# GpSimd's weight subtraction in four pieces a unit, in the mixers and the first feed-forward units

## The chip, the cores and the metric

The kernel runs on one core of a Trainium2 chip. The core has five engines with queues of their own: TensorE (PE in the profile; PEld is its weight load), VectorE (DVE), ScalarE (ACT), GpSimd (POOL) and SyncE (SP, which here only issues DMAs). They meet at semaphores. The metric is the device time of one execution in microseconds, the median of several runs.

## The reference, cut to what matters

A diffusion backbone of four layers works on 256 latent tokens and 256 context tokens of width 1024. The token mixer of layer i is of kind i % 3: windowed attention (layers 0 and 3), latent attention (layer 1), a bidirectional linear recurrence (layer 2). Each mixer is followed by a gated feed-forward with a convolution of three taps. Everything is float32.

```
for layer in range(DEPTH):                       # 4
    kind, idx = layer % N_MIXERS, layer // N_MIXERS
    ...
    h_lat = modulate(rmsnorm(x, norm1[layer]), sh1, sc1)
    h_ctx = modulate(rmsnorm(ctx, norm1[layer]), csh1, csc1)
    ...                                          # y_lat, y_ctx = mixer(h_lat, h_ctx, its weights)
    x = x + g1 * y_lat
    x = x + g2 * conv_ffn(modulate(rmsnorm(x, norm2[layer]), sh2, sc2),
                          ffn_w_up[layer], ffn_conv_w[layer], ffn_conv_b[layer], ffn_w_down[layer])
    if with_ctx_out:                             # the same for ctx, in all layers but the last
        ...

def conv_ffn(h, w_up, conv_w, conv_b, w_down):
    gate, val = jnp.split(h @ w_up, 2, axis=-1)
    gate = depthwise_conv(gate, conv_w, conv_b, FFN_CONV // 2)
    return (jax.nn.silu(gate) * val) @ w_down
```

## The kernel before

**Products in three terms.** Float32 matrix products are made of three products in the format fp32r. Each operand is split into a high part (the value rounded to fp32r) and a low part (what is left); `mm3` (L221 to L227) adds high times high, high times low and low times high in PSUM, lines L224, L225 and L226.

**Weight units.** The weights come as 367 units in the order of `unit_plan`, nearly all of 128 x 1024 numbers (the latent attention has 15 of 384 to 864 columns). `load` issues one DMA of a unit into a buffer `raw` (three of them) on SP's queue; `convert` lets ScalarE write the high part `whi` (L214) and GpSimd subtract it from `raw` to get the low part `wlo` (L215). `whi` and `wlo` have three buffers each. So GpSimd's queue is almost only this: 367 subtractions, 44 subtractions of 128 x 256 for a part of the normalized activations (`h_lo`, L439), and a few small ones.

**Stages.** The span is, in order: the first mixer (windowed attention, to about 280 us), the feed-forward of layer 0 (to 622), latent attention (to 930), feed-forward 1 (to 1300), the recurrence (1340 to 1510), feed-forward 2 (1550 to 1920), the last windowed attention (to 2085) and the last feed-forward. `out_tail` (L451) ends each stage: it adds the last projection to the residual `x` (L449), and interleaves with it the next norm: squares and their sums (L410, L412), the reciprocal root `rsqrt` (L262 to L271, some fifteen VectorE operations on 2 to 16 columns), the normalized activations `hn` (L434) and their split into `h_hi` (L435) and `h_lo` (L441 on VectorE, L439 on GpSimd).

**Feed-forward.** `ffn` does 22 column blocks f; each has an up unit for the gate (`fug`) and one for the value (`fuv`), and the down units `fdn` follow in groups. The first three up units (`lead`) are multiplied half by half while the norm is still being finished. From f = 1 on, VectorE also makes the modulation of the next layer, 1024 columns an operation (L373, `junk<-mw,cbc`).

**Order.** Each engine's program is fixed when the kernel is built, and each engine works in that order. A tracker of the tile framework puts a semaphore wait on each instruction that reads what another engine writes, and it tells parts of a tile apart: a reader waits for the writers of the columns that it reads.

Of the kernel before, what the change touches and what calls it, by code (L numbers as in the profile page):

```python
# [15 lines left out]
ALU = mybir.AluOpType  # L16
# [95 lines left out]
def hybrid_kernel(ctx: ExitStack, tc: tile.TileContext, xT, cc, ccT, W, modwa, modwb, modw, colv, rowv, tabs, band, out, depth=DEPTH, dbg=None):  # L112
    nc = tc.nc
# [16 lines left out]
    f32 = lambda ap: ap.bitcast(F32)  # L130
# [73 lines left out]
    def load(key):  # L204
        off, w = offs[key]
        raw = raw_p.tile([128, 1024], F32, tag="raw", name="raw")[:, :w]
        nc.sync.dma_start(raw, bass.AP(tensor=W.tensor, offset=W.offset + off, ap=[[w, 128], [1, w]]))
        return raw

    def convert(raw):  # L210
        w = raw.shape[-1]
        hi = w_p.tile([128, 1024], F32R, tag="whi", name="whi")[:, :w]
        lo = w_p.tile([128, 1024], F32R, tag="wlo", name="wlo")[:, :w]
        nc.scalar.activation(hi, raw, AF.Copy)  # L214
        nc.gpsimd.tensor_tensor(lo, raw, f32(hi), op=ALU.subtract)  # L215
        return hi, lo

    def unit(key):
        return convert(load(key))

    def mm3(ps, terms, start=True, stop=True, **kw):  # L221
        n = len(terms)
# [229 lines left out]
    def out_tail(l, part, keys, per, src, t0, nxt, bank):  # L452
# [10 lines left out]
        for z, key in enumerate(keys):  # L463
            wt = unit(key)
            for m, w in cols(z, wt):
                proj_cols(l, part, m, w, src, slice(t0, T) if z < split_at else CTX[1], bank)
                if z >= split_at:
                    held.append((m, w))
# [21 lines left out]
    def half_proj(l, key, m, units, src, t0):  # L490
        if m % 2 == 0:
            units[0] = unit((*key, 0, m // 2))
        wh, wl = units[0]
        o = (m % 2) * 4
        proj_cols(l, 16, m, [(wh[:, (o + k) * 128:(o + k + 1) * 128], wl[:, (o + k) * 128:(o + k + 1) * 128])
                             for k in range(4)], src, slice(t0, T), fl_ps)
# [26 lines left out]
    def swa(l, i, q0, nm, nxt, first=None):  # L523
# [12 lines left out]
        def proj(c, ps, lead=False, hook=None):  # L536
            late, done = [], []
            for q in range(4):
                wt = hook(q, done) if hook else None
                wh, wl = wt or unit(("qkv", i, c, q))  # L540

                def part(b, q=q, wh=wh, wl=wl):
                    return mm3(ps[b], [(hblk(hi, 2 * q + z, b), hblk(lo, 2 * q + z, b), wh[:, z * 512:(z + 1) * 512],
                                        wl[:, z * 512:(z + 1) * 512]) for z in range(2)], start=q == 0, stop=q == 3)

                if lead and q < 3:
                    part(0)
                    part(1)
                    late += [lambda part=part, b=b: part(b) for b in (2, 3)]
                    if q < 2:  # L550
                        continue
                    for f in late:
                        f()
                    continue
                for b in ps:
                    op = part(b)
                done.append(op)
# [611 lines left out]
    def first(q, done):  # L1169
        with ExitStack() as order:  # L1170
            if q > 1:
                order.enter_context(tc.issue_after(done[q - 2]))
            if q > 0:
                order.enter_context(tc.issue_after(applied[q - 1]))
            mod0_lead(q, raws[q])
            wt = convert(wkv[q] if q < 3 else load(("qkv", 0, 0, q)))
        for z, s in enumerate((1, 0)):
            op = nm.apply(s, rbs[z], range(2 * q, 2 * q + 2))
        applied.append(op)
        return wt  # L1180
# [151 lines left out]
```

## Time and profile before

| | |
|---|---|
| median of 3 runs | 2292.8 us (2292.27 to 2296.81) |
| profiled execution, its own time | 2288.72 us |
| its span, first to last instruction | 2286.9 us |
| granted TensorE clock, mean | 0.979 |
| busy: PE, DVE, ACT, POOL | 2133.3, 1628.4, 1031.6, 956.4 us |

The profiled execution is one run of its own; around its span lie 1.8 us. Busy times of PE count matmuls that overlap in a pipeline, so a busy PE is not PE at its peak. Starts are microseconds from the span's start.

### The profile page before, as it was taken

What the parts mean: (1) busy time and instruction counts of PE and PEld (TensorE: products, weight loads), DVE (VectorE), ACT (ScalarE), POOL (GpSimd) and SP (SyncE); (2) the same over time, 40 slices, a digit from 0 to 9 for tenths busy, and PEclk for the clock granted to TensorE, in tenths of its full rate; (3) what the DMA queues carried; (4) which work ended last, traced back from release to release, by engine and by line L of the source; (5) the groups of instructions that cost most, each with busy time, mean ns of one, the idle gap of its engine ahead of it and who ended that gap; (6) DMA issues with size and microseconds to landing.
All of it is one profiled execution on the core that took longest, in us unless ns stands there. A gap on an engine that the chain in (4) does not pass through costs nothing.

```text
span 2286.9 us, 32497 instructions
## 1 busy us (share of the span) xinstructions
PE 2133.3 (93%) x12084; PEld 1772.5 (78%) x12084; DVE 1628.4 (71%) x3342; ACT 1031.6 (45%) x1850; POOL 956.4 (42%) x418
## 2 busy tenths in 40 slices
PE   6989999999989998899999988899999999898999
PEld 5656788888877666888888876688888887677999
DVE  4678779777776887687879789857964457885333
ACT  4466553232246775433232356635333224575544
POOL 3231145454533002354545433344544443414887
PEclk9999999999999999999999998899999999999999
DMA  8433135555522001155556422223655552303555
GB/s 301 183 120 130 38 119 190 173 172 166 176 88 66 21 29 56 54 196 175 174 175 186 128 71 68 74 83 111 193 182 172 174 162 83 102 32 98 185 184 157
DMA packets 83884, 300.11 MB, mean 131 GB/s; under 512 B 11152, under 2 KB 12816, under 8 KB 81296
## 3 DMA queue, kind: packets, MB, share of 16 engines
q1 hardware_dynamic: 83728, 298.05, 40.2%
q8 instruction: 95, 1.56, 0.3%
q14 instruction: 61, 0.50, 0.1%
HBM read 296.97 MB, written 1.05 MB: 130 GB/s over the span
## 4 chain that ended last, share of the span: by engine, by line
PE 73%; DVE 19%; ACT 4%; issue 2%; DMA 2%; POOL 1%; SPq 0%; ACTq 0%; DVEq 0%; POOLq 0%
PE fl L225 8%; PE fl L226 8%; PE fl L224 8%; PE mm L224 7%; PE mm L226 7%; PE mm L225 7%; PE mo L225 4%; PE mo L224 4%; PE mo L226 4%; PE tp L226 2%; PE tp L224 2%; PE tp L225 2%; PE mo L697 2%; PE tp L691 2%; PE mm L884 2%
## 5 line engine op out<-in xcount | busy, mean ns | idle before, releaser
L215 POOL TENSOR_TENSOR wlo<-raw,whi 128x1024 fp32r<-128x1024 f32 (+3 forms) x367 | 922.4, 2516 | 1247.9 <-ACT whi L214 1212.4
L214 ACT ACTIVATE whi<-raw 128x1024 fp32r<-128x1024 f32 (+3 forms) x367 | 382.4, 1043 | 480.6 <-PE tp L225 189.9
L373 DVE SCALAR_TENSOR_TENSOR junk<-mw,cbc 128x1024 bf16<-128x1024 f32 x256 | 456.6, 1784 | 24.1 <-DMA mw<-in_modw_dram 15.8
L224 PE MATMUL fl<-h_hi,whi 128*128 128x512 f32 (+1 forms) x832 | 298.7, 360 | 10.4 <-DVE lam L958 5.9
L226 PE MATMUL fl<-h_hi,wlo 128*128 128x512 f32 (+1 forms) x832 | 298.9, 360 | 3.6 <-POOL wlo L215 3.6
L225 PE MATMUL fl<-h_lo,whi 128*128 128x512 f32 (+1 forms) x832 | 298.9, 360 | 0.4 <-POOL h_lo L439 0.2
L224 PE MATMUL mm<-h_hi,whi 128*128 128x512 f32 (+1 forms) x768 | 271.1, 353 | 3.1 <-ACT h_hi L435 2.7
L226 PE MATMUL mm<-h_hi,wlo 128*128 128x512 f32 (+1 forms) x768 | 270.1, 352 | 3.7 <-POOL wlo L215 3.7
L225 PE MATMUL mm<-h_lo,whi 128*128 128x512 f32 (+1 forms) x768 | 269.6, 352 | 0.8 <-POOL h_lo L439 0.2
L1109 DVE SCALAR_TENSOR_TENSOR conv<-mm,colt,conv 128x510 f32<-128x510 f32 (+1 forms) x88 | 59.8, 680 | 190.3 <-ACT conv L1107 190.3
L224 PEld LDWEIGHTS fl<-h_hi,whi 128*128 128x128 f32 x832 | 158.8, 192 | 34.2 <-issue 6.0
L1113 ACT ACTIVATE conv<-conv 128x512 f32<-128x512 f32 (+1 forms) x88 | 51.0, 580 | 287.4 <-DVE conv L1111 287.3
L226 PEld LDWEIGHTS fl<-h_hi,wlo 128*128 128x128 f32 x832 | 159.0, 191 | 27.2 <-POOL wlo L215 4.6
L225 PEld LDWEIGHTS fl<-h_lo,whi 128*128 128x128 f32 x832 | 159.1, 191 | 23.5 <-POOL h_lo L439 0.6
L224 PE MATMUL mo<-g_hi,whi 128*128 128x256 f32 (+1 forms) x488 | 165.4, 339 | 9.8 <-DVE x L449 6.8
L224 PEld LDWEIGHTS mm<-h_hi,whi 128*128 128x128 f32 x768 | 147.2, 192 | 23.3 <-ACT h_hi L435 3.7
L225 PE MATMUL mo<-g_lo,whi 128*128 128x256 f32 (+1 forms) x488 | 164.6, 337 | 0.4 <-DVE g_lo L259 0.4
L226 PEld LDWEIGHTS mm<-h_hi,wlo 128*128 128x128 f32 x768 | 146.8, 191 | 23.1 <-POOL wlo L215 4.3
L226 PE MATMUL mo<-g_hi,wlo 128*128 128x256 f32 (+1 forms) x488 | 164.4, 337 | 0.0
L225 PEld LDWEIGHTS mm<-h_lo,whi 128*128 128x128 f32 x768 | 146.3, 191 | 20.7 <-POOL h_lo L439 1.4
L449 DVE SCALAR_TENSOR_TENSOR x<-mo,modc,x 128x256 f32<-128x256 f32 x212 | 95.3, 477 | 84.2 <-PE mo L226 83.9
L224 PEld LDWEIGHTS mo<-g_hi,whi 128*128 128x128 f32 x488 | 93.1, 191 | 21.9 <-DVE x L449 7.5
(313 smaller groups left out, 4443.9 us busy)
## 6 DMA issues: line engine op xcount, KB each, us to landing
raw<-in_W_dram SPq DMA_DIRECT2D x352, 512.0 KB, 3.6
mw<-in_modw_dram SPq DMA_DIRECT2D x144, 512.0 KB, 4.2
mw<-in_modwa_dram SPq DMA_DIRECT2D x8, 1024.0 KB, 15.2
mw<-in_modwb_dram SPq DMA_DIRECT2D x16, 512.0 KB, 4.5
mw<-in_modwb_dram SPq DMA_DIRECT2D x8, 1024.0 KB, 8.6
cbc<-in_cc_dram SPq DMA_DIRECT2D x3, 1024.0 KB, 6.1
raw<-in_W_dram SPq DMA_DIRECT2D x8, 384.0 KB, 2.9
x<-in_xT_dram SPq DMA_DIRECT2D x8, 256.0 KB, 4.9
```

Of the source, the lines that this page charges most:

```text
L214: nc.scalar.activation(hi, raw, AF.Copy)
L215: nc.gpsimd.tensor_tensor(lo, raw, f32(hi), op=ALU.subtract)
L224: nc.tensor.matmul(ps, ah, bh, start=start and i == 0, stop=False, **kw)
L225: nc.tensor.matmul(ps, ah, bl, start=False, stop=False, **kw)
L226: op = nc.tensor.matmul(ps, al, bh, start=False, stop=stop and i == n - 1, **kw)
L373: nc.vector.scalar_tensor_tensor(junk, raw, 1.0, cbc[:, s], op0=ALU.mult, op1=ALU.mult, accum_out=modc[l][:, s, m:m + 1])
L449: nc.vector.scalar_tensor_tensor(X[m][:, half], ps[:, half], modc[l][:, s, part + m:part + m + 1], X[m][:, half], op0=ALU.mult, op1=ALU.add)
L691: nc.tensor.transpose(pp[:, c:c + 128], P[z][:, (2 * kp + kk) * 128:(2 * kp + kk + 1) * 128], ident)
L697: nc.tensor.matmul(po[r], v[0][:, kb, p * 128 + 64 * z:p * 128 + 64 * z + 64], pt[:, kp, (kk * 2 + z) * 128:(kk * 2 + z + 1) * 128], start ...
L884: nc.tensor.matmul(ps[:, c], d["q"][:96, 2 * hp + z, bc], d["k"][:96, 2 * hp + z, :nk], start=True, stop=True)
L1109: op = nc.vector.scalar_tensor_tensor(y3[:, :, 1:], g3[:, :, :255], cw[:, l, 0, f:f + 1], y3[:, :, 1:], op0=ALU.mult, op1=ALU.add)
L1113: nc.scalar.activation(y[:, t0:], y[:, t0:], AF.Silu)
```

## The change

`convert` gets a number of parts. With four parts the subtraction on GpSimd is issued as four instructions over a quarter of the columns each (three instructions where the width is not a multiple of 512); the high part stays one instruction on ScalarE. `unit` asks for one part for the down units (`fdn`) and for up units with f over 1, and for four elsewhere; the first units of layer 0 go through `convert` with its default, four.

```
-    def convert(raw):
+    def convert(raw, parts=4):
         w = raw.shape[-1]
         hi = w_p.tile([128, 1024], F32R, tag="whi", name="whi")[:, :w]
         lo = w_p.tile([128, 1024], F32R, tag="wlo", name="wlo")[:, :w]
         nc.scalar.activation(hi, raw, AF.Copy)
-        nc.gpsimd.tensor_tensor(lo, raw, f32(hi), op=ALU.subtract)
+        step = w // (parts if w % 512 == 0 else min(parts, 3))
+        for c in range(0, w, step):
+            cs = slice(c, c + step)
+            nc.gpsimd.tensor_tensor(lo[:, cs], raw[:, cs], f32(hi[:, cs]), op=ALU.subtract)
         return hi, lo
 
     def unit(key):
-        return convert(load(key))
+        return convert(load(key), 1 if key[0] == "fdn" or key[0][0] == "f" and key[2] > 1 else 4)
```

119 of the 367 units are cut: 104 into four pieces and 15 into three. 248 stay whole, 62 in each feed-forward. All later lines of the changed kernel stand three lines further down.

On GpSimd's queue, from the first mixer over the feed-forward of layer 0 to the latent attention, the kernel before has these rows (`wlo` is the low part of a unit, `mask` a table of the attention):

```order
L215 TENSOR_TENSOR wlo<-raw,whi 128x1024 x3
L439 TENSOR_TENSOR h_lo<-hw,h_hi 128x256 x2
L577 CAST mask<-mk 128x512 x2
L215 TENSOR_TENSOR wlo<-raw,whi 128x1024 x21
L439 TENSOR_TENSOR h_lo<-hw,h_hi 128x256 x6
L215 TENSOR_TENSOR wlo<-raw,whi 128x1024 x63
L215 TENSOR_TENSOR wlo<-raw,whi 128x864 x2
L215 TENSOR_TENSOR wlo<-raw,whi 128x576
```

In the changed kernel the same stretch of GpSimd's queue reads:

```order
L218 TENSOR_TENSOR wlo<-raw,whi 128x256 x12
L442 TENSOR_TENSOR h_lo<-hw,h_hi 128x256 x2
L580 CAST mask<-mk 128x512 x2
L218 TENSOR_TENSOR wlo<-raw,whi 128x256 x84
L442 TENSOR_TENSOR h_lo<-hw,h_hi 128x256 x6
L218 TENSOR_TENSOR wlo<-raw,whi 128x256 x4
L218 TENSOR_TENSOR wlo<-raw,whi 128x1024 x62
L218 TENSOR_TENSOR wlo<-raw,whi 128x288 x6
L218 TENSOR_TENSOR wlo<-raw,whi 128x192 x3
```

Nothing has moved past anything else; each unit of the mixer stands as its pieces, and in the feed-forward one unit of the 63 is cut behind the `h_lo` (three more, the `lead`, stand ahead of them).

On TensorE, where the first two pairs of row blocks of the first projection are multiplied (`mm` and `fl` are PSUM banks), the kernel before has, with the semaphores that each row waits for:

```order
L224 MATMUL mm<-whi,h_hi 128x512 [waits Activation_49]
L225 MATMUL mm<-wlo,h_hi 128x512 [waits Pool_49]
L226 MATMUL mm<-whi,h_lo 128x512 [waits DVE_49]
L224 MATMUL mm<-whi,h_hi 128x512 [waits Activation_49]
L225 MATMUL mm<-wlo,h_hi 128x512
L226 MATMUL mm<-whi,h_lo 128x512 [waits DVE_49]
```

And the changed kernel has there:

```order
L227 MATMUL mm<-whi,h_hi 128x512 [waits Activation_49]
L228 MATMUL mm<-wlo,h_hi 128x512 [waits Pool_49]
L229 MATMUL mm<-whi,h_lo 128x512 [waits DVE_49]
L227 MATMUL mm<-whi,h_hi 128x512 [waits Activation_49]
L228 MATMUL mm<-wlo,h_hi 128x512 [waits Pool_49]
L229 MATMUL mm<-whi,h_lo 128x512 [waits DVE_49]
```

The order is the same; a matmul waits for the pieces with the columns that it reads, so the second product has a wait of its own. The rows of VectorE, ScalarE and SP keep their order everywhere; on TensorE one product is swapped with its neighbours in two feed-forward beginnings.

## Rows read from the trace of the kernel before

**Rows 1.** The page: busy times and shares; the chain that ended last, by engine.
```profile
PE 2133.3 (93%) x12084; PEld 1772.5 (78%) x12084; DVE 1628.4 (71%) x3342; ACT 1031.6 (45%) x1850; POOL 956.4 (42%) x418
...
PE 73%; DVE 19%; ACT 4%; issue 2%; DMA 2%; POOL 1%; SPq 0%; ACTq 0%; DVEq 0%; POOLq 0%
```
**Rows 2.** Busy time by stretch: us, then PE, PEld, DVE, ACT, POOL (instructions).
```profile
60.00:200.00 140.00, 124.16 (x808) 83.53 (x808) 105.50 (x360) 80.87 (x197) 31.27 (x13) 0.98 0.42 151
...
320.00:620.00 300.00, 300.00 (x1326) 248.37 (x1325) 240.12 (x338) 94.93 (x116) 150.75 (x56) 1.00 0.55 179
...
1357.00:1510.00 153.00, 129.14 (x511) 102.47 (x511) 136.21 (x128) 95.25 (x122) 59.38 (x22) 0.90 0.25 73
```
**Rows 3.** VectorE in time, 284 to 316 us: start, length, instruction [idle before].
```profile
287.85 0.17 DVE L265 TENSOR_SCALAR rs_i<-rs_v 128x2 int32<-128x2 int32 x1
288.05 2.30 DVE L266 TENSOR_SCALAR rs_y<-rs_i 128x2 int32<-128x2 int32 x1
290.39 0.16 DVE L268 TENSOR_TENSOR rs_t<-rs_y 128x2 f32<-128x2 f32 x1
290.58 0.16 DVE L269 SCALAR_TENSOR_TENSOR rs_t<-rs_t,rs_v 128x2 f32<-128x2 f32 x1
290.66 0.42 DVE L412 TENSOR_TENSOR P<-P 128x256 f32<-128x256 f32 x1
...
293.48 2.20 DVE L412 TENSOR_TENSOR P<-P 128x256 f32<-128x256 f32 x1 [0.42 <-ACT P L410]
295.61 0.47 DVE L434 SCALAR_TENSOR_TENSOR hn<-x,scale,tp 128x256 f32<-128x256 f32 x1
...
305.91 0.61 DVE L270 SCALAR_TENSOR_TENSOR rs_y<-rs_t,rs_y 128x2 f32<-128x2 f32 x1
```
**Rows 4.** GpSimd in the same stretch.
```profile
287.93 2.40 POOL L215 TENSOR_TENSOR wlo<-raw,whi 128x1024 fp32r<-128x1024 f32 x1 [10.73 <-ACT whi L214]
293.02 2.38 POOL L215 TENSOR_TENSOR wlo<-raw,whi 128x1024 fp32r<-128x1024 f32 x1 [2.69 <-ACT whi L214]
...
305.77 0.73 POOL L439 TENSOR_TENSOR h_lo<-hw,h_hi 128x256 fp32r<-128x256 f32 x1 [1.43 <-ACT hw L438]
```
**Rows 5.** VectorE by line: ns min/median/max, first and last start.
```profile
L449 DVE SCALAR_TENSOR_TENSOR x<-mo,modc,x x212: 466/476/485, 338.8 to 2283.8; 128x256 f32<-128x256 f32 x106
...
L373 DVE SCALAR_TENSOR_TENSOR junk<-mw,cbc x256: 1204/1226/3299, 329.3 to 1892.0; 128x1024 bf16<-128x1024 f32 x128
```
**Rows 6.** VectorE in time: the first and the last blocked operation of cut units.
```profile
26.16 1.29 DVE L441 SCALAR_TENSOR_TENSOR h_lo<-hn,modc,h_hi 128x256 fp32r<-128x256 f32 x1
...
2086.59 0.35 DVE L265 TENSOR_SCALAR rs_i<-rs_v 128x2 int32<-128x2 int32 x1
```
**Rows 7.** GpSimd by line and shape: busy us, mean ns.
```profile
L215 POOL TENSOR_TENSOR wlo<-raw,whi 128x1024 fp32r<-128x1024 f32 x352 | 897.8, 2553 | 1207.5 <-ACT whi L214 1172.4 <-DVE h_lo L441 12.1 <-PE mo L226 8.0
L439 POOL TENSOR_TENSOR h_lo<-hw,h_hi 128x256 fp32r<-128x256 f32 x44 | 32.3, 735 | 71.8 <-ACT hw L438 71.7
```
**Rows 8.** GpSimd, then VectorE, 115 to 122 us: two units back to back.
```profile
116.15 4.75 POOL L215 TENSOR_TENSOR wlo<-raw,whi 128x1024 fp32r<-128x1024 f32 x2 [17.67 <-ACT whi L214]
...
116.44 2.13 DVE L268 TENSOR_TENSOR rs_t<-rs_y 128x8 f32<-128x8 f32 x1
...
119.17 1.75 DVE L269 SCALAR_TENSOR_TENSOR rs_t<-rs_t,rs_v 128x8 f32<-128x8 f32 x1
```
**Rows 9.** GpSimd, then VectorE, 1433 to 1443 us, in the recurrence.
```profile
1435.01 5.93 POOL L215 TENSOR_TENSOR wlo<-raw,whi 128x1024 fp32r<-128x1024 f32 x2 [6.22 <-ACT whi L214]
...
1435.92 2.77 DVE L1028 TENSOR_SCALAR th<-ex 128x1024 f32<-128x1024 f32 x1
1438.73 3.30 DVE L1029 SCALAR_TENSOR_TENSOR ex<-ex 128x1024 f32<-128x1024 f32 x1
```
**Rows 10.** Waits of TensorE for GpSimd: us in total, times, longest.
```profile
PE mm L226 <- POOL wlo L215: 3.7, 3, 1.2
...
PE fl L226 <- POOL wlo L215: 3.6, 2, 1.9
```

## The prediction

> **What bounds the kernel now.** The page comes first: TensorE is busy 93% of the span, and the chain that ended last runs over TensorE for 73% and over VectorE for 19%; GpSimd holds 1% of it and is busy 42% [rows 1]. By that, cutting a GpSimd instruction should change nothing. The shares are means over unlike stages, so the second view is busy time by stretch: in the middle of a feed-forward TensorE is busy 300.00 of 300 us, but in the first mixer 124 of 140, and in the recurrence 129 of 153 while VectorE has 136 [rows 2]. What VectorE loses in the mixers and around the norms can cost time; in the middle of a feed-forward it can't.
>
> The third view is VectorE's timeline beside GpSimd's. At 288.05 an operation on two columns takes 2.30 us, where its neighbours take 0.16 and 0.17 [rows 3]. A subtraction of a unit began on GpSimd at 287.93 and took 2.40 [rows 4]: the VectorE operation ends when the subtraction does, at 290.35 against 290.33. The same at 293.48: 2.20 us instead of 0.42, with a subtraction from 293.02 to 295.40 [rows 3, 4]. A short subtraction blocks for its own length only: one from 305.77 to 306.50 holds an operation of 0.15 us for 0.61 [rows 3, 4]. Which operations are held is plain from their spread: L449, with an input in PSUM, has 466 to 485 ns in all 212 cases, L373, with both inputs in SBUF, 1204 to 3299 [rows 5]. So a GpSimd subtraction has something for its whole length that a VectorE operation with its operands in SBUF needs too.
>
> I count an operation as blocked when it overlaps a subtraction and is over 0.15 us longer than the quick ones of its shape. Beside units that the change cuts there are 95, from 26.16 to 2086.59 us [rows 6], and together they lose 167 us; 80 of them, with 141 us, lie on the chain. That is the stock from which a gain could come: 1.76 us an operation.
>
> **What the change does, part by part.** (1) *Price of a piece.* A subtraction of 256 columns takes 0.735 us, one of 1024 some 2.40 [rows 4, 7]. Two back to back take 4.75 us, so each next one begins 0.05 before the other's end [rows 8]. Four pieces thus take 4 x 0.735 - 3 x 0.05 = 2.8 us: 0.4 more a unit, about 0.135 for each of the 342 added instructions, 46 us on an engine that is idle 58% of the time [rows 1]. By itself that is hidden. It is not hidden where VectorE would be held by the additional 0.4.
>
> (2) *Who goes next.* No row shows four pieces, but rows 8 have two units back to back: the operation that started at 116.44 ended at 118.57, just behind the first unit's end (116.15 + 2.40 = 118.55), and did not wait for the second, which ended at 120.90. The next contending operation, at 119.17, then waited for that end. In the recurrence, too, the two engines alternate: unit, L1028, unit, L1029 [rows 9]. So I take it that a VectorE operation waits for the rest of one piece, and the next contending operation can meet the next piece.
>
> (3) *Sum over the blocked operations.* With that rule there are three sorts. Alone: at 293.48 the first piece would end at 293.75, so the 0.42 us operation ends at 294.2 instead of 295.7; the next, L434 at 0.47 us, does not contend [rows 3]; about 1.2 to 1.5 stay. In a run: from 288.05 on L266, L268, L269 and L412 all contend, and each meets a piece; L412 starts about 287.93 + 2.8 + 3 x 0.16 = 291.2 instead of 290.7, a loss of 0.3 to 0.5. Long ones: L1028 and L1029 lose 2.1 us each now [rows 9]; each would lose 0.7, and the six pieces left fall to later operations, or into a pause in which VectorE waits for ScalarE. Going through all 95 in order, with VectorE's pauses and the arrival of units kept as they are relative to its work, I get in us gained: first mixer to 240 us -4.0, its end and the first norm (240 to 316) +5.3; latent attention to 850 -2.5, its end (850 to 966) +3.5; the way into the recurrence +4.1, the recurrence itself +12.4, its end +1.9; the norm and the beginning of the last attention +5.5, its middle -0.7, its end +3.0. Sum +28.5. With 0.10 or 0.22 us for an added piece it is 38 or 12: these are the ends of this term. On the chain lie 141 of 167 us, 84%: 24 us.
>
> (4) *TensorE's first low part.* It waits for `wlo` five times, 7.3 us in all [rows 10]. With pieces the first product can go 2.40 - 0.735 = 1.7 us earlier, so these waits nearly vanish; TensorE then soon waits for VectorE's norm instead, so I count a third, 2 us.
>
> (5) *What costs nothing.* The changed program has 192 more TensorE instructions with a wait on GpSimd. In the middle of a feed-forward, where such waits stand for every unit, TensorE has no idle time [rows 2]; if GpSimd were late, each wait would show. The buffers `raw` are freed by the last piece, 0.4 us later; GpSimd sits idle before 352 units for 1207 us, nearly all of it waiting for ScalarE's `whi` [rows 7], so that stays hidden. The two swapped products keep their 0.12 us each.
>
> Sum: 24 + 2 = 26 us. The profiled execution took 2288.7, so 2262.7; it was 4.1 under the median of the runs shown, so I forecast 2266.8 by that median, in round numbers 2267.
>
> **The rivals.** *Bigger gain.* VectorE's pauses don't stay: where it waits for ScalarE or TensorE, these waited for it before, and later pieces fall into pauses. If each blocked operation on the chain kept only the rest of one piece (80 x (1.76 - 0.45) = 105 us at most) and half of that reached the end, the gain would be 50 us: 2243. Against it: rows 3 show runs of contending operations right behind a blocked one.
>
> *No change.* The blocked time is on the chain, but TensorE, busy 129 of 153 us in the recurrence and 124 of 140 in the first mixer [rows 2], takes up the slack when VectorE gets faster, and the runs lose what the lone ones win. Within 4.6 us (0.2%, about what a measurement of this kernel can tell): 2288 to 2297.
>
> *Slower: GpSimd keeps the hold from piece to piece.* All four pieces stand ahead of a VectorE operation in their queue. If GpSimd went on to its next piece while the operation waits, it would wait for 2.8 us instead of 2.4, and the 80 on the chain would lose 0.4 each, 32 us: 2325. It decides from two pieces on: an operation passed over once waits up to 1.4, not far under the 1.76 of now. Rows 8 and 9 speak against it. The Trainium skill ("SBUF — State Buffer", section "Who interferes with whom") says that whoever issues first gets the shared port pair for the whole instruction and the other fully blocks. Read strictly by issue order, that rule gives this rival and its 2325; rows 8, where the operation got in ahead of a unit that had long been queued, bear out the rule for one instruction, but not that reading for a row of them.
>
> **How the numbers follow.** The sum above holds with a chance of 0.55; its own range, from the ends of term 3 (10 to 32 us on the chain, and 2 more), is 2259 to 2281. The bigger gain has 0.13, a small gain of 5 to 10 us 0.07, no change 0.15, slower 0.10. So faster by over 0.2%: 0.75; same 0.15; slower 0.10. The range leaves out most of the slower rival and the farther half of the bigger gain: 2240 to 2294.
>
> **What would show it.** Right: GpSimd's pieces near 0.73 us and four a unit in 2.8 or a little more; the operation at 288.05 and its fellows down from 2.3 to under 0.9 us; the longest of L412 from 2.4 to about 1.2; the recurrence shorter by about ten us; TensorE's waits for `wlo` under 3 us; the middle of the feed-forwards unchanged at 300 us. Wrong: single VectorE operations still at 2.3 us and longer beside cut units (GpSimd keeps its hold); pieces that grow to 1.5 us and more in the recurrence and TensorE waiting for `wlo` there (VectorE starves GpSimd); or blocked time that falls while the stages keep their length (the path was elsewhere).

## The result, and the profile after

The changed kernel takes 2239.5 us (median of 4 runs, 2239.5 to 2246.5) where the kernel before took 2293.1 beside it: a ratio of 0.977 with a 95% interval of 0.975 to 0.979, 53.5 us less. In a later group of runs it took 2241.5 (4 runs, 2239.0 to 2245.5) against 2293.9: 0.9775, 0.976 to 0.979. The forecast was 2267 with a range down to 2240: the sign and the mechanism held, the size was twice the forecast, and the time lies half a microsecond under the range.

The page of the changed kernel, its engines and the chain that ended last:

```profile
PE 2120.5 (95%) x12084; PEld 1762.9 (79%) x12084; DVE 1572.0 (70%) x3342; ACT 1033.3 (46%) x1850; POOL 1046.0 (47%) x760
...
PE 76%; DVE 16%; ACT 4%; DMA 2%; issue 1%; POOL 1%; SPq 0%; ACTq 0%; DVEq 0%
```

Against [rows 1] GpSimd has 342 instructions and 90 us more, VectorE 56 us less, and TensorE, for the same 12084 products, 12.8 us less. The span went from 2286.9 to 2237.8, so TensorE's idle time (span less busy) went from 153.6 to 117.3. The 49.1 us of the two profiles are thus 36.3 of idle time and 12.8 of products that ran quicker.

Busy time by stretch of the changed kernel (us, then PE, PEld, DVE, ACT, POOL with instructions, granted clock). Each stretch begins and ends at the product of TensorE with which the stretches of the kernel before do:

```profile
58.60:196.60 138.00, 125.71 (x808) 85.06 (x808) 101.54 (x360) 81.29 (x197) 39.52 (x54) 0.97 0.43 153
309.70:609.70 300.00, 300.00 (x1325) 248.45 (x1325) 240.09 (x338) 94.94 (x116) 151.92 (x56) 1.00 0.55 179
...
649.70:684.70 35.00, 32.91 (x228) 30.38 (x227) 29.03 (x79) 22.43 (x57) 19.30 (x26) 1.00 0.20 62
1306.30:1326.80 20.50, 18.50 (x128) 16.97 (x128) 19.08 (x48) 11.41 (x21) 11.98 (x16) 1.00 0.20 60
1326.80:1468.60 141.80, 123.31 (x512) 98.15 (x511) 123.63 (x132) 94.08 (x120) 93.40 (x84) 0.94 0.27 79
```

The first, second and fifth answer to [rows 2]: the first mixer 2.0 us shorter, the middle of the feed-forward 300.00 as before, the recurrence 11.2 shorter. To the third and fourth answer these two of the kernel before:

```profile
660.00:700.00 40.00, 35.54 (x228) 33.03 (x227) 32.37 (x77) 22.50 (x57) 16.89 (x13) 0.91 0.18 55
1330.00:1357.00 27.00, 20.87 (x128) 18.68 (x128) 23.77 (x52) 11.45 (x21) 9.97 (x7) 0.87 0.20 59
```

Five and 6.5 us went there. In both the granted clock was 0.91 and 0.87 before and is 1.00 now, and the same 228 and 128 products take 2.6 and 2.4 us less.

VectorE of the changed kernel where [rows 3] stand, start and length:

```profile
279.34 0.17 DVE L268 TENSOR_SCALAR rs_i<-rs_v 128x2 int32<-128x2 int32 x1
279.54 0.64 DVE L269 TENSOR_SCALAR rs_y<-rs_i 128x2 int32<-128x2 int32 x1
280.22 0.66 DVE L271 TENSOR_TENSOR rs_t<-rs_y 128x2 f32<-128x2 f32 x1
280.91 0.67 DVE L272 SCALAR_TENSOR_TENSOR rs_t<-rs_t,rs_v 128x2 f32<-128x2 f32 x1
...
284.85 0.55 DVE L415 TENSOR_TENSOR P<-P 128x256 f32<-128x256 f32 x1 [0.42 <-ACT P L413]
285.31 0.47 DVE L437 SCALAR_TENSOR_TENSOR hn<-x,scale,tp 128x256 f32<-128x256 f32 x1
```

GpSimd in the same stretch, as in [rows 4]:

```profile
279.42 3.07 POOL L218 TENSOR_TENSOR wlo<-raw,whi 128x256 fp32r<-128x256 f32 x4 [8.40 <-ACT whi L214]
284.38 3.00 POOL L218 TENSOR_TENSOR wlo<-raw,whi 128x256 fp32r<-128x256 f32 x4 [1.89 <-ACT whi L214]
```

The 2.30 us operation on two columns is 0.64 now, but its followers pay 0.66 and 0.67: this run meets a piece each. The lone operation of 2.20 us is 0.55.

### The profile page after: what moved, and what is told of

Its sections match the earlier page's. It is cut to its first block, busy times and chain, and to the rows that moved or that the text cites. A ratio compares the mean times of both kernels' runs of the same rounds, so it can differ in the third digit from the quotient of the medians.

```text
span 2237.8 us, 32872 instructions
## 1 busy us (share of the span) xinstructions
PE 2120.5 (95%) x12084; PEld 1762.9 (79%) x12084; DVE 1572.0 (70%) x3342; ACT 1033.3 (46%) x1850; POOL 1046.0 (47%) x760
## 4 chain that ended last, share of the span: by engine, by line
PE 76%; DVE 16%; ACT 4%; DMA 2%; issue 1%; POOL 1%; SPq 0%; ACTq 0%; DVEq 0%
PE fl L228 9%; PE fl L229 8%; PE fl L227 8%; PE mm L227 7%; PE mm L229 7%; PE mm L228 7%; PE mo L228 4%; PE mo L227 4%; PE mo L229 4%; PE tp L227 3%; PE tp L229 2%; PE tp L228 2%; PE mo L700 2%; PE mm L887 2%; PE tp L694 2%
## 5 line engine op out<-in xcount | busy, mean ns | idle before, releaser
L218 POOL TENSOR_TENSOR wlo<-raw,whi 128x256 fp32r<-128x256 f32 (+3 forms) x709 | 1011.4, 1448 | 1121.6 <-ACT whi L214 1086.0
L376 DVE SCALAR_TENSOR_TENSOR junk<-mw,cbc 128x1024 bf16<-128x1024 f32 x256 | 457.6, 1788 | 24.3 <-DMA mw<-in_modw_dram 14.7
L452 DVE SCALAR_TENSOR_TENSOR x<-mo,modc,x 128x256 f32<-128x256 f32 x212 | 95.4, 477 | 85.9 <-PE mo L229 85.6
```

Source lines behind the costliest of these rows:

```text
L218: nc.gpsimd.tensor_tensor(lo[:, cs], raw[:, cs], f32(hi[:, cs]), op=ALU.subtract)
L376: nc.vector.scalar_tensor_tensor(junk, raw, 1.0, cbc[:, s], op0=ALU.mult, op1=ALU.mult, accum_out=modc[l][:, s, m:m + 1])
L452: nc.vector.scalar_tensor_tensor(X[m][:, half], ps[:, half], modc[l][:, s, part + m:part + m + 1], X[m][:, half], op0=ALU.mult, op1=ALU.add)
```

## Experiments

Held time below is counted as in the prediction (VectorE operations over 0.15 us longer than the quick ones of their shape in the kernel before, beside a subtraction of weights); L376, which runs in the feed-forwards (L373 before), is left out. Idle is TensorE's. Half-clock is the sum of the stretches with a granted clock of 0.5, the lower of TensorE's two levels (1.2 GHz); in most kernels the last such stretch runs some 2 us past the span and is counted whole. All but the first two columns are from the profiled execution; diffs are against the changed kernel.

| kernel | median us | ratio to before, 95% interval | span | TensorE busy | idle | held | half-clock |
|---|---|---|---|---|---|---|---|
| before | 2293.1 | 1 | 2286.9 | 2133.3 | 153.6 | 180 | 98 |
| changed | 2239.5 | 0.975 to 0.979 | 2237.8 | 2120.5 | 117.3 | 122 | 70 |
| changed, again | 2241.5 | 0.976 to 0.979 | 2243.7 | 2125.4 | 118.3 | 119 | 85 |
| last columns first | 2251.6 | 0.979 to 0.983 | 2249.8 | 2133.0 | 116.8 | 116 | 96 |
| last columns first, again | 2246.2 | 0.977 to 0.982 | 2242.2 | 2125.3 | 116.9 | 114 | 79 |
| attention units whole | 2259.4 | 0.984 to 0.987 | 2258.5 | 2129.2 | 129.3 | 139 | 87 |
| two pieces | 2258.3 | 0.983 to 0.987 | 2261.6 | 2130.1 | 131.5 | 149 | 91 |
| eight pieces | 2236.9 | 0.971 to 0.977 | 2233.8 | 2122.8 | 111.0 | 94 | 74 |
| recurrence only | 2268.1 | 0.986 to 0.991 | 2273.4 | 2126.9 | 146.5 | 158 | 88 |
| other feed-forward units only | 2282.3 | 0.992 to 0.996 | 2279.0 | 2128.7 | 150.3 | 175 | 95 |
| all units in four | 2232.5 | 0.972 to 0.974 | 2227.1 | 2118.6 | 108.5 | 115 | 67 |
| all units in eight | 2249.1 | 0.978 to 0.982 | 2251.5 | 2146.2 | 105.3 | 84 | 74 |
| eight in the mixers, four in the feed-forwards | 2214.2 | 0.964 to 0.967 | 2213.1 | 2112.4 | 100.7 | 90 | 53 |

### Is it the shorter hold, or the earlier first columns?

The pieces are issued from the last columns to the first, so the hold is as short but TensorE's first columns come last.

```
-        for c in range(0, w, step):
+        for c in range(w - step, -1, -step):
```

> The changed kernel with the pieces of a unit issued in the opposite order, the last columns first. TensorE's first product of a unit reads the first columns, so it now waits for the whole unit again, while the holds on VectorE stay short. Theory A (the gain is VectorE's shorter blocked time: 167 us before, 108 after beside the cut units): VectorE's blocked time stays near 108 us, TensorE waits for GpSimd some 7 us again in five places, and the time is 2240 to 2247 us. Rival B (the gain is TensorE getting the first low parts earlier): most of the gain is lost, 2275 us or more.

TensorE's waits for GpSimd's low parts in this kernel (us in total, times, longest):

```profile
PE fl L229 <- POOL wlo L218: 7.4, 3, 3.7
...
PE mm L229 <- POOL wlo L218: 4.9, 3, 2.2
...
PE mo L229 <- POOL wlo L218: 3.4, 1, 3.4
...
PE mm L228 <- POOL wlo L218: 0.6, 1, 0.6
...
PE fl L228 <- POOL wlo L218: 0.2, 1, 0.2
```

They are 16.5 us, where the kernel before had 7.3 [rows 10] and the changed one has none. Yet TensorE's idle time is 116.8, that of the changed kernel; the 12 us between the two profiles are its busy time, 2133.0 against 2120.5. At 2251.6 the kernel stands far nearer to theory A than to B: most of the gain is the hold. Whether the 12 us are a cost of the late first columns or chance of the clock was asked again, beside the changed kernel itself.

> The changed kernel itself, profiled once more, for what of its gain comes back in a second execution. Theory A (of the 49 us about 36 are idle time of TensorE and 13 its higher granted clock, both effects of the shorter stops): idle 114 to 121 us, busy 2117 to 2125 us, half-clock stretches 62 to 80 us. Rival B (the clock's part is chance of one execution): idle the same, busy back at 2128 to 2134 us, half-clock stretches over 85 us.

> The four pieces issued from the last columns to the first, profiled once more beside the changed kernel. Theory A (the low parts' late first columns make TensorE stop about 9 us more, and these stops cost clock): TensorE busy 2128 to 2135 us, 2248 to 2256 us. Rival B (the 12 us between it and the changed kernel were chance of the clock in one group of executions): busy 2117 to 2125 us, 2238 to 2246 us.

The changed kernel's idle time came back (118.3), its busy time only in part: 2125.4, just over theory A's bound and 8 us under before, not 13; the half-clock stretches, 85 us, stand at B's bound. So it is between the two. The other came out at 2125.3 with 16 us of waits, and at 2246.2: just over rival B's bounds.

The mean granted clock is on record for every run, and it tells more than the two profiles. It was 0.975 to 0.981 in the 23 runs of the kernel before beside these experiments, 0.982 to 0.986 in the 8 runs of the changed kernel, and 0.979 to 0.986 in the 9 with the reversed order. Each run of the changed kernel stands above each run of the kernel before, so its higher clock is no chance of one execution; how much of it a single execution gets varies, and with it the clock's part of the gain, 8 and 13 us in the two profiles. By the ratios to the kernel before, the reversed order is 9 and 5 us behind the changed kernel, with intervals that just overlap each time. Its idle time is the same, and its clock (0.981 in the mean, against 0.984 and 0.979) lies between: what the order is worth, from nothing to some 9 us, seems to be clock.

### Do the stages with long runs lose?

The sum in the prediction had the attention mixers' long stretches as losses. Here their units stay whole (with one part as `convert`'s default, too).

```
-        return convert(load(key), 1 if key[0] == "fdn" or key[0][0] == "f" and key[2] > 1 else 4)
+        return convert(load(key), 1 if key[0] == "fdn" or key[0][0] == "f" and key[2] > 1 or key[0] in ("qkv", "mdn", "muq", "mkv") or key[0] in ("swo", "mwo") and key[-2] == 0 else 4)
```

> The changed kernel, but the units that are used inside the attention mixers (the projections and the first half of the output projection of layers 0, 1 and 3) are whole again; cut stay the second half of the output projection, the recurrence and the first feed-forward units. The ledger of the prediction gives these stages a loss by the cut (-4.0 to 240 us, -2.5 to 850 us, -0.7 in the last attention), so by it this kernel is 6 to 7 us faster than the changed one, 2233 us. The theory after the result (blocked time fell there too: losses are taken up by pauses, gains are not) says that the cut gained about 2 us before 240, 6 to 7 in the latent attention up to 850 and 1 to 2 in the last attention, so this kernel is 8 to 12 us slower than the changed one, 2248 to 2252 us.

It went the other way from the prediction's sum, and further than the other theory said: 2259.4, 20 us slower than the changed kernel, with 17 us more of held time, 12 more of idle and 9 more of TensorE's busy time. These units gain.

### How does it go with the number of pieces?

```
-    def convert(raw, parts=4):
+    def convert(raw, parts=2):
```

(and 2 for 4 in `unit`; then 8 for 4 in both, and six where the width is no multiple of 512.)

> Two pieces of 512 columns (about 1.3 us each) in the same units in place of four. Theory A: a blocked operation waits for the rest of one piece; the mean wait rises from 0.46 to about 0.8 us, the blocked time beside these units lies about halfway between 167 and 108 us, 130 to 140, and the time about halfway, 2258 to 2270 us. Rival (what counts is only that a subtraction can be interrupted once): nearly the full gain, 2245 us or less.

> The 119 units in eight pieces (six where the width is no multiple of 512) in place of four. Theory A (a held VectorE operation pays the rest of the piece it meets, and halves of 2048 columns went from about 180 us of held time to 149 with two pieces and 122 with four): a further step of the same kind, held time 95 to 110 us, TensorE idle 7 to 15 us less than in the changed kernel, 2225 to 2236 us. Rival B (runs of VectorE operations already meet one piece each, so that shorter pieces only add pieces to meet, and 400 more instructions at 0.13 us make GpSimd's low parts late): held time not under 115 us, 2240 to 2255 us.

With one, two, four and eight pieces the held time is 180, 149, 122 and 94 us: each halving takes off about 28. The idle time is 153.6, 131.5, 117.3 and 111.0: the first step returns 22 us, the last 6. (The units have 1024 columns; the 2048 in the second expectation is a slip.) With eight, the held time is one us under theory A's range, the idle time fell by 6.3 us where 7 to 15 were expected, and the 2236.9 lie between the two theories. The recurrence is 5 us shorter than in the changed kernel although TensorE now waits 6.0 us for low parts there; the beginnings of the first three feed-forwards, with their first up units in eight, are some 2 us longer each than in the kernel before. Two pieces went as theory A had it.

### Do stages stand for themselves?

```
-        return convert(load(key), 1 if key[0] == "fdn" or key[0][0] == "f" and key[2] > 1 else 4)
+        return convert(load(key), 4 if key[0][0] == "l" else 1)
```

(with one part as `convert`'s default), and the opposite half of the feed-forwards:

```
+        return convert(load(key), 4 if key[0] == "fdn" or key[0][0] == "f" and key[2] > 1 else 1)
```

(here `convert`'s default stays four, so the first four units of layer 0 are cut as well: 252 units, not the 248 of the expectation.)

> Only the units of the recurrence in four pieces, all others whole. Theory A (stages stand for themselves, what a cut unit gives is given in its own stage): the stretch from 1270 to 1510 us of the kernel before is 15 to 22 us shorter, every other stretch within 2 us of before, 2271 to 2278 us. Rival B (the gain of a stage hangs on where the stages ahead of it left the units): under 10 us in that stretch, 2283 us or more.

> The opposite half: only the 248 feed-forward units that the change leaves whole are cut in four, the 119 of the change stay whole. Theory A (the two sets add up: all units in four gave 60 us, the 119 alone 49): 8 to 13 us off, 2280 to 2285 us, all of it at the ends of the feed-forward blocks and the norms behind them. Rival B (they give only together, since the norm behind a feed-forward block runs beside units of the next mixer): within 4 us of the kernel before.

Both went by theory A. The first is 3 us under theory A's range. In its profile (an execution of 2275.2, 7 us over the median) 17.6 us come from the recurrence and the way into it (the same stretch, from 1270 on, gives 20.0 in the changed kernel); of the other stretches the first 30 us are 2.6 us longer, those from 30 to 140 us 1.0 and the last attention 1.9, the way out of the recurrence is 1.6 shorter, and the rest is within 0.2. In the second the held time of L376 fell from 146 to 42 us, and the kernel gained 13: those 104 us lie beside a TensorE that never waits. In its profile, 7.9 us shorter than that of before, the gain came at the norms behind the first three feed-forwards, some 2 to 4 us each, and 2 us came from the four units of layer 0.

### What is the best cut?

```
+        return convert(load(key), 4)
```

> All 367 units in four (or three) pieces, also those of the middle of the feed-forwards. Theory A: there TensorE has no idle time, VectorE's blocked time (146 us of L373 before) is off the path, so the time stays within 3 us of the changed kernel, 2237 to 2243 us. Rival: GpSimd, 50% busy there and alternating with the 1.2 us operations L373, gets late with the low parts, TensorE waits for it, and the time rises by 10 us or more.

> All 367 units in eight pieces (six where the width is no multiple of 512). Theory A: as with four pieces in all units (2232 us) and a further 7 to 15 us less, 2217 to 2226 us. Rival B (some 1,600 added instructions at 0.13 us are 210 us more of GpSimd, which turns late in the feed-forward blocks and makes TensorE wait there): 2235 to 2270 us.

All units in four is faster than the changed kernel, 2232.5, beyond what was expected of it. All units in eight was 67 us ahead of the kernel before at the end of the last mixer and lost 32 of them in the last feed-forward. Its busy times there, 2050 to 2210 us:

```profile
2050.00:2210.00 160.00, 160.00 (x1160) 159.07 (x1159) 44.08 (x98) 68.73 (x96) 159.94 (x384) 1.00 0.53 159
```

The same with all units in four:

```profile
2050.00:2210.00 160.00, 159.93 (x1333) 159.73 (x1333) 53.02 (x116) 78.67 (x113) 157.61 (x225) 1.00 0.62 185
```

GpSimd does 384 pieces in 159.94 us, 3.33 us a unit of eight; in four it does a unit in 2.80, and 56 units in 160 us are one each 2.86. So four pieces just keep step with TensorE there and eight don't: 1160 products instead of 1333, though TensorE is called busy throughout. That is rival B, in the one feed-forward where TensorE uses up units so fast; in the middle of the first it was 56 units in 300 us [rows 2], and the other three feed-forwards lost at most 2 us each with eight. So the next kernel has eight in the mixers and four in all feed-forwards (the first four units of layer 0 have `convert`'s default, four):

```
-        step = w // (parts if w % 512 == 0 else min(parts, 3))
+        step = w // (parts if w % 512 == 0 else min(parts, 6 if parts == 8 else 3))
...
+        return convert(load(key), 4 if key[0] == "fdn" or key[0][0] == "f" else 8)
```

> Eight pieces (six where the width is no multiple of 512) in the mixers' units, four (three) in all feed-forward units. Theory A (stages stand for themselves; eight pieces gave 67 us by the end of the last mixer and then lost 32 in the last feed-forward block, where GpSimd was busy almost throughout): that loss goes, the rest stays, 2218 to 2226 us. Rival B (eight pieces give nothing that can be measured beyond four): 2228 to 2236 us, as with four pieces in all units.

It takes 2214.2 us (2212.0 to 2215.0), under theory A's range, and is the fastest of all: 79.7 us less than before. Eight pieces in the first three feed-forwards beside four in the last were not tried.

```profile
PE 2112.4 (95%) x12084; PEld 1758.0 (79%) x12084; DVE 1445.8 (65%) x3342; ACT 1039.2 (47%) x1850; POOL 1341.1 (61%) x1885
```

## Why the prediction was right in kind and short in size

**Right: price and turn (terms 1 and 2).** Four pieces take 3.0 to 3.1 us in the norm shown above, against 2.8 worked out. GpSimd has 90 us more, not the 46 of term 1: VectorE now holds its pieces in turn, and the 440 pieces of 256 columns take 0.84 us in the mean against 0.735. That stays hidden; TensorE waits for no low part.

```profile
L218 POOL TENSOR_TENSOR wlo<-raw,whi 128x256 fp32r<-128x256 f32 x440 | 357.4, 844 | 569.2 <-ACT whi L214 538.9 <-issue 12.5 <-PE mo L700 6.3
```

VectorE gets in behind each piece. The recurrence shows it longest: here VectorE, then GpSimd, at the place of [rows 9].

```profile
1401.60 1.12 DVE L1031 TENSOR_SCALAR th<-ex 128x1024 f32<-128x1024 f32 x1
1402.74 1.65 DVE L1032 SCALAR_TENSOR_TENSOR ex<-ex 128x1024 f32<-128x1024 f32 x1
```

```profile
1400.61 7.87 POOL L218 TENSOR_TENSOR wlo<-raw,whi 128x256 fp32r<-128x256 f32 x8 [4.33 <-ACT whi L214]
```

2.77 and 3.30 us became 1.12 and 1.65, and the eight pieces of two units take 7.87 us because VectorE's operations lie between them. Single pieces grow to 1.8 us in the recurrence. That is one half of a sign of being wrong; the other half, TensorE waiting for `wlo` there, did not come. The rival in which GpSimd keeps its hold is out.

**The step that failed: term 3, the sum over the blocked operations.** It forecast 28.5 us less held time, the trace has 58.5. By stage, in us (time is the stretch's gain in the first profile and in the second):

| stage (starts of before) | forecast | held time less | time less |
|---|---|---|---|
| to 240 | -4.0 | 6.1 | 4.1, 0.8 |
| 240 to 316 | 5.3 | 6.7 | 6.3, 6.3 |
| latent attention to 850 | -2.5 | 4.2 | 5.7, 3.7 |
| 850 to 966 | 3.5 | 7.0 | 7.0, 5.9 |
| 966 to 1270 | 0 | 0 | -1.6, -2.1 |
| 1270 to 1357 | 4.1 | 4.5 | 8.7, 7.2 |
| recurrence, 1357 to 1510 | 12.4 | 14.4 | 11.3, 11.6 |
| 1510 to 1600 | 1.9 | 6.3 | 2.3, 1.8 |
| 1880 to 1960 | 5.5 | 5.6 | 2.1, 2.1 |
| 1960 to 2070 | -0.7 | 0.3 | 0.7, 1.8 |
| 2070 to 2110 | 3.0 | 3.4 | 2.8, 4.2 |
| sum | 28.5 | 58.5 | 49.4, 43.3 |

The stretches that are not listed differ from before by at most 0.4 us. In six stages the sum was good to 2 us. It failed where it booked losses, to 240 us and in latent attention, and at 850 to 966 and 1510 to 1600. No stage's held time grew. The price of one meeting was right: beside cut units 236 operations are held for 108.5 us, 0.46 each, where the prediction reckoned 0.45. The number of meetings was too high: 167 less 28.5 us at 0.46 would be 301.

The prediction's own example, the run of operations from 288.05 on, shows how. It was to lose 0.3 to 0.5 us, with L412 starting 3.3 us behind the beginning of the subtraction. Behind that L412 the kernel before has, and the changed kernel has, on VectorE and then on GpSimd:

```profile
291.07 0.48 DVE L449 SCALAR_TENSOR_TENSOR x<-fl,modc,x 128x256 f32<-128x256 f32 x1
```

```profile
281.50 0.41 DVE L415 TENSOR_TENSOR P<-P 128x256 f32<-128x256 f32 x1
281.83 0.68 DVE L273 SCALAR_TENSOR_TENSOR rs_y<-rs_t,rs_y 128x2 f32<-128x2 f32 x1
282.43 0.47 DVE L452 SCALAR_TENSOR_TENSOR x<-fl,modc,x 128x256 f32<-128x256 f32 x1
```

```profile
281.51 0.98 POOL L218 TENSOR_TENSOR wlo<-raw,whi 128x256 fp32r<-128x256 f32 x1
```

L412 started 2.73 us behind the subtraction (290.66 less 287.93), L415 starts 2.08 behind it (281.50 less 279.42). Three operations meet a piece each and end with it, so the 0.16 us of each, which the prediction added, don't come on top. L415 gets in ahead of the fourth piece and is not lengthened; the piece is, to 0.98 us. L273 then pays for that piece, and the next operation, L452, starts 3.01 us behind the subtraction where L449 started 3.14 behind it: the run gained 0.13 us.

Latent attention shows the rest. VectorE, then GpSimd, of the kernel before:

```profile
662.54 2.03 DVE L265 TENSOR_SCALAR rs_i<-rs_v 128x2 int32<-128x2 int32 x1
...
667.33 1.86 DVE L270 SCALAR_TENSOR_TENSOR rs_y<-rs_t,rs_y 128x2 f32<-128x2 f32 x1
```

```profile
662.49 2.06 POOL L215 TENSOR_TENSOR wlo<-raw,whi 128x864 fp32r<-128x864 f32 x1 [10.60 <-ACT whi L214]
667.12 2.05 POOL L215 TENSOR_TENSOR wlo<-raw,whi 128x864 fp32r<-128x864 f32 x1 [2.57 <-ACT whi L214]
```

And of the changed one:

```profile
652.21 0.78 DVE L268 TENSOR_SCALAR rs_i<-rs_v 128x2 int32<-128x2 int32 x1
653.02 0.74 DVE L269 TENSOR_SCALAR rs_y<-rs_i 128x2 int32<-128x2 int32 x1
653.80 0.72 DVE L271 TENSOR_TENSOR rs_t<-rs_y 128x2 f32<-128x2 f32 x1
...
656.88 0.64 DVE L273 SCALAR_TENSOR_TENSOR rs_y<-rs_t,rs_y 128x2 f32<-128x2 f32 x1
657.44 0.41 DVE L415 TENSOR_TENSOR P<-P 128x256 f32<-128x256 f32 x1
658.32 0.48 DVE L437 SCALAR_TENSOR_TENSOR hn<-x,scale,tp 128x256 f32<-128x256 f32 x1 [0.47 <-PE tp L427]
```

```profile
652.16 2.34 POOL L218 TENSOR_TENSOR wlo<-raw,whi 128x288 fp32r<-128x288 f32 x3 [10.60 <-ACT whi L214]
656.66 2.63 POOL L218 TENSOR_TENSOR wlo<-raw,whi 128x288 fp32r<-128x288 f32 x3 [2.16 <-ACT whi L214]
```

The first unit's pieces meet three operations and cost what the whole one did. The second unit meets the last contending operation of the run for 0.64 instead of 1.86; its other pieces lie beside L415, which is not lengthened, a pause, and L437, which reads PSUM and is not held. The sum had pushed VectorE's work along behind the pieces with its pauses kept, and so into more pieces. That the pauses, as waits for something else, also take up what a run loses is argued, not shown: VectorE's idle time fell from 15.2 to 13.6 us in 640 to 700, but from 25 to 240 us it rose by 3, and over the span it went from 658.5 to 665.8.

**And the share.** The prediction let 84% of the held time return because 84% lay on the chain. Of 58.5 us, 36.3 returned as idle time of TensorE, 62%; with two and eight pieces it is 70% and 49%. At 1510 to 1600 and 1880 to 1960 together 11.9 us of held time gave 4.4 or less.

**A term that was not in the sum: the clock.** The half-clock stretches went from 98 us to 70 (85 in the second profile), and TensorE's busy time fell by 12.8 us (8); every run of the changed kernel has the higher clock, as told above. One place, busy times of the kernel before from 661 us on:

```profile
661.00:668.50 7.50, 5.50 (x45) 5.08 (x43) 6.82 (x18) 2.94 (x6) 3.44 (x2) 1.00 0.18 54
668.50:675.30 6.80, 6.06 (x27) 6.06 (x28) 4.47 (x10) 2.79 (x6) 1.46 (x2) 0.50 0.16 58
```

And the same place of the changed kernel:

```profile
651.00:658.40 7.40, 6.00 (x49) 5.59 (x48) 6.34 (x20) 2.88 (x5) 4.08 (x5) 1.00 0.16 54
658.40:665.20 6.80, 6.71 (x52) 6.23 (x51) 6.30 (x17) 4.94 (x11) 3.80 (x7) 1.00 0.32 103
```

TensorE's stops there, before and after, in the brackets:

```profile
669.24 1.22 PE L424 MATMUL tp<-tabt,rs_y 128*128 128x128 f32 x4 [2.20 <-DVE rs_y L270]
```

```profile
657.58 0.71 PE L427 MATMUL tp<-tabt,rs_y 128*128 128x128 f32 x4 [0.98 <-DVE rs_y L273]
```

Before, TensorE stopped for 2.2 us at the held L270, to 669.2; during that stop its granted clock fell to 0.50 and stood there for 6.8 us, and 27 products took the time in which the changed kernel, stopped there for 1.0 us, does 52 at 1.00. That the shorter stop is what kept the clock up is argued from such places and from the sums; no run changed the one without the other.

So 28.5 x 84% = 24 should have been 58.5 x 62% = 36, plus 8 to 13 of clock: 44 to 49, which the profiles show. The medians differ by 53.5; the profile of before was itself 4 us under its median.

**Term 4** (2 us for TensorE's first low part) can't be told from nothing: the waits are gone as forecast, and the reversed order brings up 16.5 us of them at 0 to 9 us of time. **Term 5** held for the middles of the feed-forwards; 966 to 1270 lost about 2 us that no term had. **The rivals:** the bigger gain had the number (2243), and later pieces do fall into pauses; but it had up to 105 us of held time fall away, half of it reaching the end, and left the clock out, so the number is luck in part. No change and slower are out by the time.

## What to carry to other kernels

When an engine holds another for the length of an instruction, cut the instruction until its pieces still keep step with whoever consumes them, stage by stage: of one, two, four and eight pieces, eight in the mixers with four in the feed-forwards was the fastest, and eight everywhere lost 32 us in one feed-forward. When you add up what a shorter hold gives, don't let every follower in a run meet a piece with its own time on top: here a held operation ended with its piece, one that got in ahead of a piece made the piece wait, and pieces beside pauses and PSUM readers cost VectorE nothing, so runs that were booked as losers gained. And ask what the clock did behind each stop: here a stop of two microseconds came with seven at half speed, which no view of waits lists.

## What the runs showed of the hardware

In the last feed-forward an instruction on 256 columns costs GpSimd 0.70 us (157.61 by 225) and one on 128 columns 0.42 (159.94 by 384): 0.28 for 128 columns and some 0.13 for the instruction, which agrees with the 0.135 worked out from [rows 4, 7]. The two engines take turns even in a row of eight pieces (7.87 us above), and the hold works both ways: a piece that began behind L415 took 0.98 us. The Trainium skill ("SBUF — State Buffer", section "Who interferes with whom") has the hold last for the whole instruction, and only for a VectorE operation in a two-port mode or with two inputs in SBUF; the trace agrees for each piece: L452, with an input in PSUM, has 467 to 486 ns in all 212 cases of the changed kernel, L376 up to 3374 beside whole units and, with all units in four, no more than 1819.
